# An encoder block on one core: late vectors in the pool's lowest place, b22 split one product earlier, and a rearranged last stage

## The chip, the core and the metric

One core of a Trainium2 chip runs the kernel. Its engines work side by side, each through its own queue in order: TensorE (PE, with weight loads PEld), VectorE (DVE), ScalarE (ACT), GpSimd (POOL), and SyncE (SP), which only issues DMAs. The metric is device time in microseconds (us), the median of the runs. Rows of the profile begin with the time from the span's start and the duration, both in us.

## The reference, cut to what matters

The block is an attention and a recurrence side by side, a projection with a layer norm, and a gated feed-forward part with a second norm. 1024 tokens, width 1024, everything float32. The change lies in the last two lines:

```python
h = layer_norm(DEEPNORM_ALPHA * h + merged @ w_o[l], ln1_g[l], ln1_b[l])
gate, up = jnp.split(h @ w_ffn_in[l], 2, axis=-1)          # 1024 -> 2 x 2816
h = layer_norm(DEEPNORM_ALPHA * h + (silu(gate) * up) @ w_ffn_out[l], ln2_g[l], ln2_b[l])
```

## The kernel before

**Products.** Every float32 operand is split into `hi` (a cast on ACT, L272) and `lo` (the source less `hi`, L276, on POOL for weights and often on DVE for activations). A block of a product is then three matmuls: hi by hi (L297), hi by lo (L298), lo by hi (L299), each 128 x 128 by 128 x 512. A large product is cut into 2 x 2 blocks, and seven block products are made instead of eight, with sums and differences of the blocks as operands (Strassen's scheme in Winograd's form). In the program's names b11, b12, b21 and b22 are the blocks of one side, t1 to t4 their sums, a11 to a22 the blocks of the other side and s1 to s4 theirs. `PRODUCTS` pairs them: product 5 is s1 by t1, 6 is s2 by t2, 3 is s4 by b22, 7 is s3 by t3, 4 is a22 by t4.

**The seam.** `phase2` makes the first norm's rows, tile after tile of 128 tokens. `turn(t)` transposes a tile (tsv) and `h1_blocks` makes the operands of the feed-forward product from it. For tokens 512 and up, b22, t3 and t4 go to DRAM (`td`, stores by `later` on SP) and `late_block` loads them back (`t_raw`) once their room is free; each of its four functions splits one quarter (`xb22`, `xt3`, `xt4`). `ffn_in` then runs 22 groups of seven products, one for each block of 128 gate and 128 up columns. The first two groups, g0 and g1, run in an order written by hand (`in_order`, which keeps each engine's instructions as the program has them). `Group.keep` copies a product out of PSUM (wkeep, L126, ACT), `Group.out` ends one with `evac`: fc (L1439), a tanh (fth, L1440), L1441. `Group.prep` splits a weight. Its sums (L100) are s1 and s2 in wsum and s3 and s4 in place in f_raw.

**Pools.** A pool of SBUF gives places to its tiles in the order in which they are first asked for. The pool `ffn` takes room that the pools of `phase2` had, and a tile whose place was another tile's waits for that tile's last readers. Its first tile is fc; its lowest place lies where tsum (t1, t2 and t4 before they are split or stored) was.

**The last stage.** `ffn_out` makes the second product. X and Z are four PSUM banks each; `OUT_ORDER` is (1, 2, 6, 5, 3, 7), and each of these six products goes over NJ = 11 weight blocks in 11 steps of 12 matmuls. A step s makes, in program order: `sums(s + 2)` on DVE, `prep(s + 2)` (w_hi on ACT, w_lo on POOL, four buffers of each), the loads listed for it in `bulk`, in p7 `later` (the split of t4: t4hi on ACT, t4lo on DVE), its 12 matmuls, one or two functions from `todo`, and `acts` for three steps on (ghi and glo, 256 KB each, three buffers of each). p3 and p7 name the products 3 and 7. `todo` holds what follows a product: adds of its banks to the rows Y, statistics, and in p7 the norms of the first four tiles. The last product, a22 by t4, goes tile by tile, four times 33 matmuls, with `late` (t4) against the operands A (704 KB for hi, 704 KB for lo, loaded by `last_acts`), and the norms and stores of the last four tiles follow.

Of the kernel before, what the change touches and what calls it, by code (L numbers as in the profile page):

```python
# [149 lines left out]
class Block:  # L150
# [1216 lines left out]
    def h1_blocks(self, pool, t, v, last=False):  # L1367

        nc = self.nc
        c = slice(128 * (t % 4), 128 * (t % 4) + 128)  # L1370

        def put(name, v):
            hi, lo = self.xb[name]
            self.split(hi[:, :, c], lo[:, :, c], v,
                       eng_lo="dve" if last else "pool")

        if t < 4:
            for i, n in enumerate(("b11", "b21")):
                put(n, v(i))
            return ()  # L1380

        def later(i, name, v):
            nc.sync.dma_start(self.td[i][:, :, c], v)

        def tmp():
            return pool.tile([128, 4, 128], F32, name="tsum", tag="tsum", bufs=3)

        def less(o, a, i, name):
            hi, lo = (z[:, :, c].bitcast(F32) for z in self.xb[name])
            nc.vector.tensor_sub(o, a, hi)  # L1390
            nc.vector.tensor_sub(o, o, lo)

        t1, t2 = tmp(), tmp()
        b12 = v(0)
        less(t1, b12, 0, "b11")
        put("t1", t1)
        b22 = v(1)

        def second():
            nc.vector.tensor_sub(t2, b22, t1)  # L1400
            put("t2", t2)

        def rest():
            later(0, "b22", b22)
            nc.vector.tensor_sub(b12, b22, b12)
            later(1, "t3", b12)
            hi, lo = (z[:, :, c].bitcast(F32) for z in self.xb["b21"])
            nc.vector.tensor_sub(t2, hi, t2)
            nc.vector.tensor_add(t2, t2, lo)
            later(2, "t4", t2)  # L1410

        return second, rest
# [9 lines left out]
    def ffn_in(self):  # L1422

        nc = self.nc
        with ExitStack() as es:
# [4 lines left out]
            C = {}  # L1430

# [54 lines left out]
            def vecs(v):  # L1486
                t = fp.tile([128, D], F32, name="ab", tag=f"ab{len(ab)}", bufs=1)
                nc.scalar.dma_start(t, bass.AP(tensor=v.tensor, offset=v.offset, ap=[[0, 128], [1, D]]))
                ab.append(t)

# [12 lines left out]
            with self.in_order():  # L1503
# [6 lines left out]
                splits = late_block(0)  # L1510
                g1.m5 = g1.keep(g1.product(5, 2, True))
                g0.prep(3)
                splits += late_block(1)
                g1.u2 = g1.keep(g1.product(6, 1, False))
                for f in splits[:4]:
                    f()
                g0.prep(7)
                g0.out(0, 1, g0.product(3, 2, False), g0.u2)
                for f in splits[4:]:
                    f()  # L1520
                g1.prep(3)
# [11 lines left out]
            ab = []  # L1533
            held = (g1.out(1, 0, g1.product(4, 1, False), None) for _ in range(1))
            for p in range(2, NF):
# [8 lines left out]
                if p == 3:  # L1544
                    for v in self.ln["1"]:
                        vecs(v)
# [93 lines left out]
    def ffn_out(self):  # L1640
# [3 lines left out]
        with ExitStack() as es:  # L1644
# [34 lines left out]
            def last_acts(t, i):  # L1679
                if i == 0:  # L1680
                    A.append([rp.tile([128, NJ, 128], F32R, name=f"a22{z}", tag=f"a22{z}", bufs=2) for z in "hl"])
                nc.sync.dma_start(A[t][i].bitcast(F32), self.gd["a22"][i][:, :, 128 * t:128 * (t + 1)])

            def sums(s):
# [6 lines left out]
                elif p == 6:  # L1691
                    W["t2", j] = t2 = self.ws.tile([128, HALF], F32, name="wt2", tag="wkeep", bufs=4)
                    nc.vector.tensor_sub(t2, b22, b11)
                elif p == 5:
                    nc.vector.tensor_add(b21, b21, b11)
                elif p == 7:
                    nc.vector.tensor_sub(b12, b22, b12)
                elif p == 3:
                    nc.vector.tensor_sub(b21, b21, b22)
# [25 lines left out]

            def moments(t):
                mv = self.tiny.tile([128, 4], F32, name="mv2", tag="bnmv", bufs=3)
# [3 lines left out]
                return mv  # L1731
# [4 lines left out]
            def whole(t):  # L1736
                y = Y[t]
                self.normalise(rp, y, y, moments(t))
                nc.gpsimd.tensor_mul(y, y, V[0])
                ends.append(t)  # L1740
                if len(ends) > 1:
                    end()

            ends, stores = [], []

            def end():
                t = ends.pop(0)
                nc.vector.tensor_add(Y[t], Y[t], V[1])
                stores.append(t)

            def finish(t, parts):
                y, (g2, b2), mv = Y[t], V, moments(t)
# [20 lines left out]
            for i in range(2):  # L1773
                at(46 + 2 * i, vector, i)
                for t in range(2):
# [6 lines left out]
            def later(j):  # L1782
                late[j] = [wb.tile([128, HALF], F32R, name=f"t4{z}", tag=f"{n}{j}", bufs=1)
                           for z, n in (("hi", "b11"), ("lo", "b12"))]
# [8 lines left out]
            for s, (p, j) in enumerate(steps):  # L1793
# [3 lines left out]
                with self.in_order():  # L1797
# [4 lines left out]
                    if p == 7 and j:  # L1802
                        later(j - 1)
                    self.out_step(s, *ready.pop(s))
                    for _ in range(2 if p == 7 else 1):
# [4 lines left out]
                if j == NJ - 1:  # L1810
# [10 lines left out]
                    if p == 3:  # L1821
                        todo = [a for r in range(4) for a in (todo[r], todo[4 + r])]
                        todo += [(whole, r) for r in range(4)]

            with self.in_order():
                later(NJ - 1)
                for f, *a in todo:
                    f(*a)
                end()
                for t in range(4, 8):  # L1830
                    stat(t, 1)
                for t in range(4):
# [3 lines left out]
                    if t < 2:  # L1836
                        for i in range(2):
                            last_acts(2 + t, i)
                    while stores:
                        store(stores.pop(0))  # L1840
                    if t in (1, 2):
                        whole(3 + t)
                        end()
# [43 lines left out]
```

## Time and profile before

| what | value |
|---|---|
| time, three runs | 2162.76 us median, 2158.73 to 2165.23 |
| the profiled execution's own time | 2162.12 us |
| its span | 2160.2 us |
| mean granted clock of TensorE | 0.984 |
| where it was below 1 in the parts touched | 0.90 in 1480 to 1550, 0.86 in 2071.3 to 2119.3 |

In the rows of windows the columns are the stretch, its length, the busy time of PE, PEld, DVE, ACT and POOL with the count of instructions, the granted clock, the DMA engines' share and GB/s. In rows of waits: who waited for whom, us in total, how often, the longest. In rows of groups: line, engine, operation, operands, shapes and count, then busy time and mean ns of one, then idle time before them and what ended it. In rows of the timeline the bracket is the idle time before the instruction and what ended it.

### The profile page before, as it was taken

To read this page: it belongs to the slowest core of one execution; us is meant where nothing else is said; L and a number is where in the kernel's file an instruction comes from. 1 tells how busy PE (TensorE), PEld (TensorE's weight loads), DVE (VectorE), ACT (ScalarE), POOL (GpSimd) and SP (SyncE) were. 2 spreads that over 40 slices of the span, in tenths; PEclk is the share of its full clock that TensorE was granted. 3 is DMA by queue.
4 is the path that set the end of the run, shared out by engine and by line. 5 is a ranking of instruction groups with operands and counts; after the bars stand their busy time and mean duration, and the time that the engine had idled before them with its cause. 6 is when DMAs were issued, how large, how long until landed. Compare 5 with 4: busy or idle time off the path is not lost.

```text
span 2160.2 us, 31223 instructions
## 1 busy us (share of the span) xinstructions
PE 2038.3 (94%) x10941; PEld 1678.3 (78%) x10941; DVE 1368.7 (63%) x2172; ACT 918.3 (43%) x1867; POOL 1199.0 (56%) x955
## 2 busy tenths in 40 slices
PE   4799999999999999989999899998899999999987
PEld 3678887878877888777888688886688888888866
DVE  7667646876459854768446623356767776759645
ACT  6544455444544436444364431243434344444221
POOL 3465653566436763556635864242667776755542
PEclk9899999999999999999999999999999999999999
DMA  5343442435334453333535764244445444467674
GB/s 205 102 127 103 139 148 92 148 118 159 118 95 140 137 164 103 127 118 124 162 98 179 237 219 145 78 142 146 132 146 180 138 167 150 160 213 277 212 223 132
DMA packets 296447, 324.20 MB, mean 150 GB/s; under 512 B 15905, under 2 KB 212834, under 8 KB 296290
## 3 DMA queue, kind: packets, MB, share of 16 engines
q1 hardware_dynamic: 288832, 296.81, 42.8%
q10 hardware_dynamic: 7458, 25.40, 3.0%
q8 instruction: 86, 1.41, 0.3%
q14 instruction: 71, 0.58, 0.1%
HBM read 211.78 MB, written 110.36 MB: 149 GB/s over the span
## 4 chain that ended last, share of the span: by engine, by line
PE 60%; DVE 6%; issue 5%; POOL 4%; DMA 2%; ACT 2%; SPq 0%; DVEq 0%; POOLq 0%; ACTq 0%
PE pj L297 13%; PE pj L298 12%; PE pj L299 12%; PE sd L297 6%; PE sd L298 6%; PE sd L299 5%; POOL w_lo L276 2%; PE sd L1091 1%; ACT p L869 1%; DVE hR L1052 1%; PE sd L905 1%; DVE p L891 1%; DVE hR L1051 1%; DMA a22l<-ga22l 0%; PE sd L696 0%
## 5 line engine op out<-in xcount | busy, mean ns | idle before, releaser
L276 POOL TENSOR_TENSOR w_lo<-wa,w_hi 128x512 fp32r<-128x512 f32 x276 | 386.7, 1409 | 277.0 <-ACT w_hi L272 255.1
L272 ACT CAST w_hi<-wa 128x512 fp32r<-128x512 f32 x276 | 170.1, 618 | 230.1 <-PE pj L298 162.3
L276 POOL TENSOR_TENSOR w_lo<-f_raw,w_hi 128x512 fp32r<-128x512 f32 x110 | 175.7, 1609 | 112.9 <-ACT w_hi L272 51.0
L297 PE MATMUL pj<-xt1hi,w_hi 128*128 128x512 f32 x268 | 108.6, 406 | 15.1 <-ACT xt1hi L272 6.6
L298 PE MATMUL pj<-xt1lo,w_hi 128*128 128x512 f32 x268 | 107.3, 400 | 4.5 <-DVE xt1lo L276 4.5
L299 PE MATMUL pj<-xt1hi,w_lo 128*128 128x512 f32 x268 | 106.7, 398 | 0.7 <-POOL w_lo L276 0.7
L299 PE MATMUL pj<-xb22hi,w_lo 128*128 128x512 f32 x268 | 104.9, 392 | 2.4 <-POOL w_lo L276 2.4
L297 PE MATMUL pj<-xb22hi,w_hi 128*128 128x512 f32 x268 | 105.7, 394 | 1.2 <-ACT xb22hi L272 1.2
L298 PE MATMUL pj<-xb22lo,w_hi 128*128 128x512 f32 x268 | 104.9, 392 | 0.2 <-DVE xb22lo L276 0.2
L531 POOL TENSOR_TENSOR wa<-wa,wa 128x512 f32<-128x512 f32 x46 | 64.5, 1402 | 72.6 <-DVE ws L530 55.5
L276 POOL TENSOR_TENSOR w_lo<-Wb,w_hi 128x512 fp32r<-128x512 f32 x47 | 66.2, 1410 | 68.0 <-ACT w_hi L272 63.7
L272 ACT CAST w_hi<-f_raw 128x512 fp32r<-128x512 f32 x110 | 67.9, 620 | 83.0 <-DVE f_raw L100 32.5
L276 POOL TENSOR_TENSOR w_lo<-ws,w_hi 128x512 fp32r<-128x512 f32 x46 | 67.3, 1468 | 63.0 <-ACT w_hi L272 60.8
L553 ACT COPY wkeep<-pj 128x512 f32<-128x512 f32 x138 | 80.4, 582 | 13.8 <-DVE evh L472 7.8
L276 POOL TENSOR_TENSOR w_lo<-wsum,w_hi 128x512 fp32r<-128x512 f32 x44 | 65.9, 1498 | 34.2 <-ACT w_hi L272 33.7
L297 PE MATMUL pj<-xb11hi,w_hi 128*128 128x512 f32 x188 | 77.0, 411 | 4.9 <-DVE wkeep L470 3.3
L456 DVE TENSOR_TENSOR evh<-wkeep,pj 128x512 f32<-128x512 f32 x48 | 32.7, 680 | 76.3 <-PE pj L299 56.2
L1043 ACT ACTIVATE hS<-hR,dec 128x128 f32<-128x128 f32 x112 | 44.5, 402 | 82.0 <-DVE hR L1052 58.5
L297 PE MATMUL pj<-xt4hi,w_hi 128*128 128x512 f32 x188 | 75.5, 402 | 2.9 <-DVE evh L445 2.9
L299 PE MATMUL pj<-xt2hi,w_lo 128*128 128x512 f32 x188 | 74.3, 395 | 3.4 <-POOL w_lo L276 3.4
L298 PE MATMUL pj<-xb11lo,w_hi 128*128 128x512 f32 x188 | 75.6, 402 | 1.0 <-DVE xb11lo L276 1.0
L530 DVE TENSOR_TENSOR ws<-wa,wa 128x512 f32<-128x512 f32 x46 | 38.5, 838 | 60.0 <-DMA wa<-in_w_in_dram 44.5
(423 smaller groups left out, 6629.5 us busy)
## 6 DMA issues: line engine op xcount, KB each, us to landing
wa<-in_w_in_dram SPq DMA_DIRECT2D x184, 256.0 KB, 3.0
f_raw<-in_w_ffn_in_dram SPq DMA_DIRECT2D x44, 512.0 KB, 4.2
Wb<-in_w_ffn_out_dram SPq DMA_DIRECT2D x40, 256.0 KB, 5.3
tg<-evh SPq DMA_DIRECT2D x32, 256.0 KB, 3.1
tg<-tg SPq DMA_DIRECT2D x16, 512.0 KB, 3.6
y<-ahs SPq DMA_DIRECT2D x16, 512.0 KB, 3.4
ah<-xt ACTq DMA_DIRECT2D x8, 512.0 KB, 6.4
rec<-hg ACTq DMA_DIRECT2D x8, 512.0 KB, 4.0
```

The source lines that it names most:

```text
L272: nc.scalar.copy(hi, src)
L276: e.tensor_sub(lo, src, hi.bitcast(F32))
L297: nc.tensor.matmul(ps, whi, xhi, start=first, stop=False, **kw)
L298: nc.tensor.matmul(ps, whi, xlo, start=False, stop=False, **kw)
L299: nc.tensor.matmul(ps, wlo, xhi, start=False, stop=last, **kw)
L456: nc.vector.tensor_add(t, add, ps)
L530: nc.vector.tensor_add(a["s1"], a["a21"], a["a22"])
L531: nc.gpsimd.tensor_sub(a["a21"], a["a11"], a["a21"])
L553: nc.scalar.copy(t, ps)
L869: nc.scalar.activation(z, z, AF.Exp, bias=N0[p, hd, tt:tt + 1], scale=QSCALE, accum_out=L0[p, hd, tt:tt + 1])
L891: nc.vector.tensor_scalar(z, z, W0[p, hd, tt:tt + 1], None, op0=OP.mult)
L1043: nc.scalar.activation(S[:, c, :], E, AF.Copy, scale=dec[:, 1, c:c + 1])
```

## The change

1. `h1_blocks` stores b22 as soon as it is there, no longer with t3 and t4.
2. `ffn_in` asks for the two vectors ab (gain and bias of the first norm, used from the fifth group on) before any other tile of its pool, and loads them from SP's queue instead of ACT's.
3. In the hand-written order b22 and t3 are split one product earlier than before, and g0's third weight is prepared before g1's product 5.
4. In the last stage the sums of product 7 are made with those of product 5; t4 is split in p3 instead of p7 (its `lo` goes to b22's place, no longer to b12's); the norm of a tile is cut into moments, normal, gained and total, which `todo` interleaves over four tiles, three functions per step of p7; A has three buffers instead of two, and the third tile's operands are loaded in p7.

```diff
         b22 = v(1)
+        later(0, "b22", b22)
...
         def rest():
-            later(0, "b22", b22)
             nc.vector.tensor_sub(b12, b22, b12)
...
             C = {}
+            ab = [fp.tile([128, D], F32, name="ab", tag=f"ab{i}", bufs=1) for i in range(2)]
...
                 splits = late_block(0)
+                g0.prep(3)
                 g1.m5 = g1.keep(g1.product(5, 2, True))
-                g0.prep(3)
                 splits += late_block(1)
-                g1.u2 = g1.keep(g1.product(6, 1, False))
                 for f in splits[:4]:
                     f()
+                g1.u2 = g1.keep(g1.product(6, 1, False))
                 g0.prep(7)
-                g0.out(0, 1, g0.product(3, 2, False), g0.u2)
                 for f in splits[4:]:
                     f()
+                g0.out(0, 1, g0.product(3, 2, False), g0.u2)
...
                 if p == 3:
-                    for v in self.ln["1"]:
-                        vecs(v)
+                    for t, v in zip(ab, self.ln["1"]):
+                        nc.sync.dma_start(t, bass.AP(tensor=v.tensor, offset=v.offset, ap=[[0, 128], [1, D]]))
...
-                    A.append([rp.tile([128, NJ, 128], F32R, name=f"a22{z}", tag=f"a22{z}", bufs=2) for z in "hl"])
+                    A.append([rp.tile([128, NJ, 128], F32R, name=f"a22{z}", tag=f"a22{z}", bufs=3) for z in "hl"])
...
                 elif p == 5:
                     nc.vector.tensor_add(b21, b21, b11)
-                elif p == 7:
                     nc.vector.tensor_sub(b12, b22, b12)
...
+            def normal(t):
+                self.normalise(rp, Y[t], Y[t], MV[t])
+
+            def gained(t):
+                nc.gpsimd.tensor_mul(Y[t], Y[t], V[0])
+
+            def total(t):
+                nc.vector.tensor_add(Y[t], Y[t], V[1])
+                stores.append(t)
...
-                for t in range(2):
+                for t in range(3):
                     at(52 + 4 * t + 2 * i, last_acts, t, i)
...
-                           for z, n in (("hi", "b11"), ("lo", "b12"))]
+                           for z, n in (("hi", "b11"), ("lo", "b22"))]
...
-                    if p == 7 and j:
-                        later(j - 1)
+                    if p == 3:
+                        later(j)
                     self.out_step(s, *ready.pop(s))
-                    for _ in range(2 if p == 7 else 1):
+                    for _ in range(3 if p == 7 else 1):
...
-                        todo += [(whole, r) for r in range(4)]
+                        for k in range(7):
+                            todo += [(f, k - n) for n, f in ((3, total), (2, gained), (1, normal), (0, moments))
+                                     if 0 <= k - n < 4]
...
-                    if t < 2:
+                    if t == 0:
                         for i in range(2):
-                            last_acts(2 + t, i)
+                            last_acts(3, i)
```

The first place is the seam. On SP, the queue before, from the store of tile 6's b22 (td_199 is b22, td_200 t3, td_201 t4):

```order
L1383 DMA td_199<-tsv 512x1x128
L1383 DMA td_200<-tsv 512x1x128
L1383 DMA td_201<-tsum 512x1x128
L1383 DMA td_199<-tsv 512x1x128
L1383 DMA td_200<-tsv 512x1x128
L1383 DMA td_201<-tsum 512x1x128
L1496 DMA t_raw<-td_199 128x512 x4
L1496 DMA t_raw<-td_200 128x512 x4
L1496 DMA t_raw<-td_201 128x512 x4
```

And the same place of the changed kernel:

```order
L1383 DMA td_199<-tsv 512x1x128 x2
L1383 DMA td_200<-tsv 512x1x128
L1383 DMA td_201<-tsum 512x1x128
L1383 DMA td_200<-tsv 512x1x128
L1383 DMA td_201<-tsum 512x1x128
L1492 DMA t_raw<-td_199 128x512 x4
L1492 DMA t_raw<-td_200 128x512 x4
L1541 DMA ab<-in_ln_g_dram 128x1024
L1541 DMA ab<-in_ln_b_dram 128x1024
L1492 DMA t_raw<-td_201 128x512 x4
```

Tile 7's b22 goes ahead of the four stores of t3 and t4, and the two vectors now stand before the last four loads.

On ACT, at the same place, before (the second row is the tanh of g0's first evacuation, the fourth the weight of g1's product 5):

```order
L1488 DMA ab<-in_ln_g_dram 128x1024
L1440 ACTIVATE fth<-fc 128x512
L126 COPY wkeep<-pj 128x512
L1488 DMA ab<-in_ln_b_dram 128x1024
L272 CAST w_hi<-wsum 128x512
L126 COPY wkeep<-sd 128x512
L1440 ACTIVATE fth<-fc 128x512
L272 CAST w_hi<-wsum 128x512
L126 COPY wkeep<-sd 128x512
L272 CAST w_hi<-f_raw 128x512
L126 COPY wkeep<-pj 128x512
L272 CAST xb22hi<-t_raw 128x512 x4
```

And of the changed kernel, from the same tanh:

```order
L1441 ACTIVATE fth<-fc 128x512
L126 COPY wkeep<-pj 128x512
L272 CAST w_hi<-wsum 128x512
L126 COPY wkeep<-sd 128x512
L1441 ACTIVATE fth<-fc 128x512
L272 CAST w_hi<-wsum 128x512
L272 CAST w_hi<-f_raw 128x512
L126 COPY wkeep<-sd 128x512
L272 CAST xb22hi<-t_raw 128x512 x4
L126 COPY wkeep<-pj 128x512
L272 CAST w_hi<-f_raw 128x512
L272 CAST xt3hi<-t_raw 128x512 x4
```

The casts of b22 moved ahead of the copy of g1's product 6 (wkeep<-pj), those of t3 ahead of the tanh that follows product 3; on DVE the halves xt3lo moved ahead of that product's fc in the same way.

The second place is product 7 of the last stage. ACT before, where the norms begin (Wb_17805 to Wb_17886 are weights of p7, the other Wb are blocks of t4, y rows of a tile):

```order
L272 CAST w_hi<-Wb_17805 128x512
L272 CAST t4hi<-Wb_17673 128x512
L320 ACTIVATE y_17888<-y_17888,mv_18963 128x1024
L320 ACTIVATE y_17915<-y_17915,mv_18970 128x1024
L272 CAST w_hi<-Wb_17832 128x512
L272 CAST t4hi<-Wb_17699 128x512
L320 ACTIVATE y_17942<-y_17942,mv_19003 128x1024
L320 ACTIVATE y_17969<-y_17969,mv_19011 128x1024
L272 CAST w_hi<-Wb_17859 128x512
L272 CAST t4hi<-Wb_17726 128x512
L272 CAST w_hi<-Wb_17886 128x512
```

And of the changed kernel:

```order
L272 CAST w_hi<-Wb_17778 128x512
L320 ACTIVATE y_17888<-y_17888,mv_18954 128x1024
L272 CAST w_hi<-Wb_17805 128x512
L320 ACTIVATE y_17915<-y_17915,mv_18981 128x1024
L272 CAST w_hi<-Wb_17832 128x512
L320 ACTIVATE y_17942<-y_17942,mv_19008 128x1024
L272 CAST w_hi<-Wb_17859 128x512
L320 ACTIVATE y_17969<-y_17969,mv_19039 128x1024
L272 CAST w_hi<-Wb_17886 128x512
```

The t4 casts left p7, and one norm's activation stands between two weights instead of two.

POOL of the changed kernel at that place (mv is a column of moments raised to -1/2, the y rows are `gained`):

```order
L1726 TENSOR_TENSOR mv_18954<-mv_18954,mhalf 128x1
L276 TENSOR_TENSOR w_lo<-Wb_17778,w_hi 128x512
L1726 TENSOR_TENSOR mv_18981<-mv_18981,mhalf 128x1
L1732 TENSOR_TENSOR y_17888<-y_17888,gb_18661 128x1024
L276 TENSOR_TENSOR w_lo<-Wb_17805,w_hi 128x512
L1726 TENSOR_TENSOR mv_19008<-mv_19008,mhalf 128x1
L276 TENSOR_TENSOR w_lo<-Wb_17832,w_hi 128x512
L1732 TENSOR_TENSOR y_17915<-y_17915,gb_18661 128x1024
L1726 TENSOR_TENSOR mv_19039<-mv_19039,mhalf 128x1
L276 TENSOR_TENSOR w_lo<-Wb_17859,w_hi 128x512
```

Before, two multiplies and two columns stood between one weight and the next; now at most one multiply does.

More of the change, by code (lines that the diff above doesn't have):

```diff
@@ L1484, in combine @@
                     parts("s4", j, s4)
[L1486 to L1489, printed above, removed]
             self.first_evac = [evac_of(FS[p]) for p in range(2)]
@@ L1532, in ffn_in @@
             combine(0, 0)
-            ab = []
             held = (g1.out(1, 0, g1.product(4, 1, False), None) for _ in range(1))
@@ L1724, in stat @@
                 nc.vector.bn_stats(S[t][:, h, :], Y[t][:, halves[h]])
+            MV = {}
             def moments(t):
-                mv = self.tiny.tile([128, 4], F32, name="mv2", tag="bnmv", bufs=3)
+                MV[t] = mv = rp.tile([128, 4], F32, name="mv2", tag=f"mv{t}", bufs=1)
                 nc.vector.bn_aggr(mv[:, 0:2], S[t])
@@ L1730, in moments @@
                 nc.gpsimd.tensor_tensor(mv[:, 2:3], mv[:, 2:3], self.mhalf[:, 0:1], OP.pow)
-                return mv
+            def normal(t):
[5 more added lines that the diff above has]
+                stores.append(t)
             def store(t, c=slice(0, D)):
                 nc.sync.dma_start(self.out[128 * t:128 * (t + 1), c], Y[t][:, c])
[L1736 to L1749, printed above, removed]
+            stores = []
             def finish(t, parts):
-                y, (g2, b2), mv = Y[t], V, moments(t)
+                moments(t)
+                y, (g2, b2), mv = Y[t], V, MV[t]
                 for s in parts:
@@ L1822, in ffn_out @@
                         todo = [a for r in range(4) for a in (todo[r], todo[4 + r])]
-                        todo += [(whole, r) for r in range(4)]
+                        for k in range(7):
+                            todo += [(f, k - n) for n, f in ((3, total), (2, gained), (1, normal), (0, moments))
+                                     if 0 <= k - n < 4]
             with self.in_order():
-                later(NJ - 1)
                 for f, *a in todo:
                     f(*a)
-                end()
                 for t in range(4, 8):
@@ L1841, in ffn_out @@
                     if t in (1, 2):
-                        whole(3 + t)
-                        end()
+                        for f in (moments, normal, gained, total):
+                            f(3 + t)
                     if t == 3:
```

## The prediction, made before the changed kernel was run

> **What bounds the kernel now.** I read the page first, then the windows, then the waits of the stretches in which PE is not full.
>
> ```profile
> span 2160.2 us, 31223 instructions
> PE 2038.3 (94%) x10941; PEld 1678.3 (78%) x10941; DVE 1368.7 (63%) x2172; ACT 918.3 (43%) x1867; POOL 1199.0 (56%) x955
> PE   4799999999999999989999899998899999999987
> GB/s 205 102 127 103 139 148 92 148 118 159 118 95 140 137 164 103 127 118 124 162 98 179 237 219 145 78 142 146 132 146 180 138 167 150 160 213 277 212 223 132
> ```
>
> PE is the bound: 94% busy, and full in most of the 40 slices. An edit can gain only where PE is not full. The change touches two such places: the seam between the output projection and the feed-forward stage (slices 27 to 29) and the last 90 us. The windows give what lies in each.
>
> ```profile
> 1480.00:1550.00 70.00, 54.03 (x202) 39.90 (x201) 47.50 (x60) 26.76 (x50) 30.58 (x22) 0.90 0.45 137
> 1970.00:2040.00 70.00, 70.00 (x311) 57.96 (x310) 51.07 (x57) 24.11 (x41) 37.44 (x28) 1.00 0.65 212
> 2066.00:2088.00 22.00, 21.79 (x94) 17.08 (x93) 13.05 (x18) 5.81 (x10) 7.76 (x6) 1.00 1.00 303
> 2071.30:2119.30 48.00, 35.91 (x133) 26.92 (x133) 28.39 (x43) 15.65 (x23) 23.12 (x16) 0.86 0.48 151
> 2119.30:2152.50 33.20, 30.71 (x134) 24.48 (x132) 14.81 (x25) 2.49 (x2) 7.33 (x5) 1.00 0.61 198
> ```
>
> The second row is PE at its pace: 70 us for 311 matmuls, 0.225 us each, so a product of 12 takes 2.70 us and one of 132 takes 29.7. The fourth row is the seventh product of the last stage, called p7 below: 132 matmuls in 48.0 us, 18.3 too long. The fifth is the last product, also 132: 33.2 us, 3.5 too long. In the first row 202 matmuls took 70 us instead of 45.5: 24.5 us lost, some of them to transposes that stay. These three are all that the change can win.
>
> **The seam.** These are the rows of the engines there.
>
> ```profile
> 1495.60 0.69 DVE L1409 TENSOR_TENSOR tsum<-tsum,xb21lo 128x512 f32<-128x512 f32 x1
> 1499.98 0.69 DVE L1439 TENSOR_TENSOR fc<-wkeep,sd 128x512 f32<-128x512 f32 x1 [3.69 <-DMA td<-tsum]
> 1503.41 0.80 PE L297 MATMUL sd<-xt1hi,w_hi 128*128 128x512 f32 x1 [5.63 <-ACT w_hi L272]
> 1503.44 1.28 POOL L276 TENSOR_TENSOR w_lo<-wsum,w_hi 128x512 fp32r<-128x512 f32 x1 [10.36 <-ACT w_hi L272]
> 1506.60 1.28 POOL L276 TENSOR_TENSOR w_lo<-wsum,w_hi 128x512 fp32r<-128x512 f32 x1 [1.88 <-ACT w_hi L272]
> 1513.25 0.51 PE L297 MATMUL pj<-xb22hi,w_hi 128*128 128x512 f32 x1 [1.25 <-ACT xb22hi L272]
> 1516.81 0.69 DVE L1439 TENSOR_TENSOR fc<-wkeep,pj 128x512 f32<-128x512 f32 x1 [1.08 <-PE pj L299]
> 1518.80 2.49 DVE L276 TENSOR_TENSOR xt3lo<-t_raw,xt3hi 128x512 fp32r<-128x512 f32 x4
> 1522.68 1.29 POOL L276 TENSOR_TENSOR w_lo<-f_raw,w_hi 128x512 fp32r<-128x512 f32 x1 [5.81 <-ACT w_hi L272]
> 1526.42 0.39 PE L297 MATMUL pj<-xt3hi,w_hi 128*128 128x512 f32 x1
> ```
>
> The first fc, in the pool's lowest place, waits for two stores that still read tsum there; DVE was free at 1495.60 + 0.69 = 1496.3. With the vectors in that place no row of the changed order waits for them: 3.7 us. Everything hung on that fc shifts with it: the product of group 1 with xt1 starts at 1499.7, its w_lo (1504.72) is there at 1501.0 and the next product's (1507.88) at 1504.2. From each w_lo ten matmuls remain: 1501.0 + 2.25 = 1503.3, and 1504.2 + 2.25 = 1506.5. The b22 split now runs one product earlier, from about 1503.9 (behind a copy of the product that ends at 1503.3), so it hides beside the product that ends at 1506.5. Group 0's third product follows without its 1.25 us: 1509.2. The t3 split starts behind one copy and one cast (about 0.6 each, as the casts quoted further down), at about 1507.7, and is ready as PE needs it: group 0's seventh ends at 1511.9.
>
> What is late next is group 1's third product. Its weights hang on the evacuation of the product that ends at 1509.2, and that evacuation now stands behind xt3lo on DVE, which ends at about 1507.7 + 0.6 + 2.5 = 1510.8. Before, from the start of that fc (1516.81) to the end of the w_lo (1523.97) was 7.2 us with 2.4 of xt3lo inside: 4.8 without. So w_lo is there at 1515.6 and the product ends at 1517.9, against 1526.42 before: 8.5 us won. Behind it the same chain of POOL's halves and weight loads sets the pace as before, shifted. Against this stand the clock's windows:
>
> ```profile
> 1488.40:1491.85 3.45, 1.73 (x6) 1.16 (x7) 2.25 (x3) 2.61 (x6) 1.74 (x2) 1.00 0.57 195
> 1491.85:1495.25 3.40, 3.40 (x9) 2.60 (x8) 3.37 (x5) 0.00 (x0) 1.23 (x1) 0.51 0.45 131
> PE pj L297 <- ACT w_hi L272: 1.1, 1, 1.1
> ```
>
> A window in which PE was half idle was followed by one at 0.51 of the clock: 9 matmuls where 15 fit. Two such idle spells stay (1497.8 to 1501.0, 1511.9 to 1515.6). Each can cost up to 1.7 us, part of it under the chain's own waits; I take 1.2 for both: **7.3 us**. Ends: 4 (both windows in full, and a later split) to 8.5. [...]
>
> The two vector loads move from ACT's queue to SP's, ahead of the last four t_raw loads. 2 x 512 KB at 303 GB/s is 3.5 us of transfer; those t_raw wait anyway for the b22 halves (about 1507) and are cast at about 1519. Behind the two on SP stand only those loads and the next weights, which wait for POOL longer. Cost 0; without that cover 3.5.
>
> **The seventh product.** Here are its waits, two matmuls behind the longest of them, two t4lo in a row on DVE, its groups and the load of a last operand.
>
> ```profile
> ACT w_hi L272 <- DVE Wb L1697: 15.5, 7, 3.4
> PE pj L297 <- ACT w_hi L272: 6.8, 2, 3.8
> PE pj L298 <- POOL w_lo L276: 4.9, 2, 2.6
> 2095.81 0.59 PE L297 MATMUL pj<-w_hi,ghi 128*128 128x512 f32 x1 [3.85 <-ACT w_hi L272]
> 2106.56 0.80 PE L297 MATMUL pj<-w_hi,ghi 128*128 128x512 f32 x1 [2.99 <-ACT w_hi L272]
> 2072.72 1.29 DVE L276 TENSOR_TENSOR t4lo<-Wb,t4hi 128x512 fp32r<-128x512 f32 x1 [1.35 <-ACT t4hi L272]
> 2077.29 1.30 DVE L276 TENSOR_TENSOR t4lo<-Wb,t4hi 128x512 fp32r<-128x512 f32 x1 [1.35 <-ACT t4hi L272]
> L276 DVE TENSOR_TENSOR t4lo<-Wb,t4hi 128x512 fp32r<-128x512 f32 x11 | 12.7, 1172 | 10.5 <-ACT t4hi L272 10.5
> L276 POOL TENSOR_TENSOR w_lo<-Wb,w_hi 128x512 fp32r<-128x512 f32 x8 | 11.2, 1396 | 14.6 <-ACT w_hi L272 14.6
> L1739 POOL TENSOR_TENSOR y<-y,gb 128x1024 f32<-128x1024 f32 x4 | 10.0, 2488 | 6.2 <-ACT y L320 6.2
> a22h<-ga22h SPq DMA_DIRECT2D x4, 704.0 KB, 6.7
> ```
>
> ACT's w_hi waits 15.5 us for the sums (L1697), which stand on DVE behind t4lo and behind norms that wait for POOL. Two steps of 10.75 us came of it. The change takes 11 sums, 11 t4hi and 11 t4lo out of p7, so a w_hi waits only for its buffer; four buffers let it run two to three steps ahead. What remains in one queue with it is one normalise on ACT and one multiply on POOL per step. A POOL step with a multiply holds 1.4 + 2.5 = 3.9 us, over 2.70, but only four of 11 are such: 11 x 1.4 + 4 x 2.5 = 25.4 of 29.7 us, beside four one-column operations. Walking POOL's order by these durations, the last w_lo ends some 26 us into p7, and its step starts at 27.0. So PE has no wait on an engine left: 18.3.
>
> What is late next is DMA. Each step loads 2 x 256 KB; the last operands, 704 KB each, come at every second step, now six of them instead of four. The window 2066 to 2088 held just this mix, at share 1.00 and 303 GB/s. Two steps are 4 x 0.262 + 0.721 = 1.77 MB, 5.84 us against 5.40: 0.44 per pair, six pairs, 2.6 us. Ends: 0, if the three buffers take it, and 6 at the 277 GB/s of the page's best slice (6.4 us per pair). **Gain 18.3 - 2.6 = 15.7.**
>
> **Where the moved work goes.** The sums go to the fifth product, the t4 splits to p3, the product before p7.
>
> ```profile
> 2039.44 2.73 DVE L1719 TENSOR_TENSOR y<-y,sd 128x512 f32<-128x512 f32 x4 [17.00 <-PE sd L299]
> 2042.09 8.80 DVE L1699 TENSOR_TENSOR Wb<-Wb,Wb 128x512 f32<-128x512 f32 x9
> L276 POOL TENSOR_TENSOR w_lo<-Wb,w_hi 128x512 fp32r<-128x512 f32 x11 | 15.6, 1422 | 14.3 <-ACT w_hi L272 14.3
> L272 ACT CAST w_hi<-Wb 128x512 fp32r<-128x512 f32 x11 | 6.8, 622 | 23.1 <-PE sd L299 23.1
> ```
>
> In the fifth product DVE idles 17.00 us before the adds that free the bank for p3; 11 sums of 0.98, the pace of the second row, are 10.8: hidden, and beyond 17 us they would hold p3. In p3 (the last two rows, 2041 to 2071) ACT idles 23.1 us and takes 11 casts of 0.62, 6.8; DVE takes 11 halves of 1.17, 12.9, beside 8.8 of sums, in 29.7. No wait is added that PE sees: t4lo needs the cast just before it and b22's w_lo of two steps ago. Cost 0 to 4, taken 0.
>
> **The last product.** Its third operand now is loaded before it starts and the fourth after its first quarter.
>
> ```profile
> PE pj L299 <- DMA a22l<-ga22l: 1.5, 1, 1.5
> PE pj L297 <- DMA a22h<-ga22h: 0.9, 1, 0.9
> 2152.51 0.69 DVE L1719 TENSOR_TENSOR y<-y,pj 128x512 f32<-128x512 f32 x1 [5.36 <-PE pj L299]
> ```
>
> The fourth pair is then issued 15 us before use and ahead of the stores. Both waits go, with the slow restarts the 3.5 us of the window; DVE idled 5.36 us before its last add, which covers 3.5. **Gain 3.5**, ends 1 and 3.5.
>
> **The sum.** The profiled execution took 2162.12 us, 1.9 more than its span and 0.6 below the median shown. 7.3 + 15.7 + 3.5 = 26.5: **2135.6 us**.
>
> **Rivals.**
> The clock stays up in the seam: 1.2 us more won, 2134.4. [...] Chance 0.14.
> DMA is worse: 6 us of stalls instead of 2.6, 2139.0; for it the full share, against it the 303 GB/s held for 22 us. 0.11.
> p3 is paced by DVE and POOL together: their operations lengthen beside each other (t4lo 1.17 on the mean, a sum 0.98, w_lo 1.42). One after the other they make 3.57 per step, 0.87 over 2.70; 9.6 in 11 steps, less two steps of lead, 4.2: 2139.8. Chance 0.09. [...]
> The norms still hold w_hi once (the change does not do what it says): one step of 10.75 stays, 8 us: 2143.6. Chance 0.07.
> The seam's gain is eaten by the chain behind it, by weight loads that wait for DMA: 2142.9. Chance 0.05.
> The slower side: in p3 ACT and DVE fall into lockstep. Before, in p7, two t4lo stood 4.57 us apart with sum and cast between them. At that period p3 loses 11 x 1.87 = 20.6 less three steps of lead, 8.1, so 12.5: 2148 (0.02). From about 5.3 us per step the time is within 0.3% of before (0.02), from 6.4 on it is slower by more, at 8 us 2186 (0.03). Against it: w_hi in p3 needs no sum.
>
> **How the numbers follow.** Forecast 0.47; the rivals as given. The range 2129 to 2147 reaches from every term at its best (8.5 + 18.3 + 3.5, 2131.8) to the norms' rival at 2143.6, each with 3 us for the scatter of the runs shown. A change of 0.3%, 6.5 us, is about what a measurement of this kernel can tell: faster 0.95, within 0.02, slower 0.03.
>
> **What would show it.** In the seam: the first fc about 0.6 us behind the last tsum, no wait of PE for xb22hi or xt3hi, and PE waiting instead for group 1's weights. In p7: no wait of ACT's w_hi for a sum, about 32 us in all, small waits of PE for ghi and glo. In the last product: no wait for a22. Wrong would be p3 longer than 30 us, a step of p7 over 5 us, or an fc that still waits for a store.

## The result, and the profile after

| | before | after |
|---|---|---|
| median of the runs, us | 2162.27 (2158.73 to 2165.23, 4 runs) | 2137.1 (2136.52 to 2137.73, 4 runs) |
| ratio | 1 | 0.9884, 95% interval 0.9867 to 0.9901 |
| profiled execution and its span, us | 2162.12, 2160.2 | 2136.52, 2134.7 |

The change made the kernel faster by 1.2%. In all medians and ratios here, three executions of the kernel before that took 35% longer or more are left out. The profiled executions differ by 25.6 us, where the prediction had 26.5. The page of the changed kernel begins so (span, busy time by engine, PE's 40 slices):

```profile
span 2134.7 us, 31233 instructions
PE 2030.1 (95%) x10941; PEld 1674.5 (78%) x10941; DVE 1375.5 (64%) x2172; ACT 916.8 (43%) x1867; POOL 1199.1 (56%) x955
PE   4799999999999999989999899999899999999998
```

PE's instructions are the same 10941. Its last slices are full now. The windows of the two places, columns as before (stretch; its length, then busy time and count of PE, PEld, DVE, ACT, POOL; clock; DMA share; GB/s):

```profile
1480.00:1550.00 70.00, 58.46 (x228) 44.62 (x228) 51.85 (x64) 31.01 (x58) 35.39 (x25) 0.93 0.51 161
2065.90:2097.00 31.10, 31.08 (x132) 24.13 (x133) 18.92 (x24) 9.41 (x12) 24.25 (x16) 1.00 0.88 273
2097.00:2127.00 30.00, 30.00 (x133) 24.60 (x131) 13.58 (x24) 2.49 (x2) 7.39 (x5) 1.00 0.49 172
```

In the seam 228 matmuls ran in 70 us instead of 202. P7 takes 31.1 us instead of 48.0, the last product 30.0 instead of 33.2. The whole list of PE's waits from 2000 us to the end is one row, and ACT's list in p7 has no sum any more (line waiting, what it waits for: us in total, times, longest):

```profile
PE sd L299 <- DMA glo<-gs4l: 0.4, 1, 0.4
...
ACT y L320 <- DVE mv L319: 6.7, 3, 3.0
ACT w_hi L272 <- PE pj L299: 5.8, 3, 2.6
ACT w_hi L272 <- PE sd L299: 2.1, 1, 2.1
```

A w_hi now waits for PE alone, that is, for a free buffer: the engine that works ahead waits for the one that is the bound. The time line of the seam, rows of DVE, PE and POOL in order of time:

```profile
1495.39 0.69 DVE L1409 TENSOR_TENSOR tsum<-tsum,xb21lo 128x512 f32<-128x512 f32 x1
1496.00 0.68 DVE L1440 TENSOR_TENSOR fc<-wkeep,sd 128x512 f32<-128x512 f32 x1
1499.43 0.50 PE L297 MATMUL sd<-xt1hi,w_hi 128*128 128x512 f32 x1 [1.88 <-ACT w_hi L272]
1509.42 3.18 DVE L276 TENSOR_TENSOR xt3lo<-t_raw,xt3hi 128x512 fp32r<-128x512 f32 x4 [0.68 <-ACT xt3hi L272]
1512.52 0.67 DVE L1440 TENSOR_TENSOR fc<-wkeep,pj 128x512 f32<-128x512 f32 x1
1515.95 0.50 PE L297 MATMUL sd<-xb22hi,w_hi 128*128 128x512 f32 x1 [2.31 <-ACT w_hi L272]
1515.97 1.66 POOL L276 TENSOR_TENSOR w_lo<-f_raw,w_hi 128x512 fp32r<-128x512 f32 x1 [5.73 <-ACT w_hi L272]
1541.60 0.50 PE L299 MATMUL pj<-xb22hi,w_lo 128*128 128x512 f32 x1 [0.88 <-POOL w_lo L276]
```

The first fc runs 0.61 us behind the last tsum, without a wait. PE waits for neither xb22hi nor xt3hi; the long wait is for the weights of group 1's third product, as foreseen. The last row is the mark that serves as the seam's end below; it stood at 1547.62.

The seam starts at 1478.3 to 1482.6 us in the runs below, whatever the kernel, so they are compared by four stretches of PE's time line: **seam**, from the first transposes that wait for y (1480.76 before, 1480.56 after) to that mark; **middle**, from there to p7's first matmul (2071.31, 2065.92); **p7**, to the first matmul with t4 (2119.39, 2097.00); **last**, to the last matmul (2152.09, 2126.70). Before: 66.9, 523.7, 48.1, 32.7. After: 61.0, 524.3, 31.1, 29.7. So -5.8, +0.6, -17.0 and -3.0 make -25.2 of the span's -25.5; 0.2 lie ahead of the seam, 0.1 behind the last matmul.

The stretches come from one profiled execution of each kernel, and kernels that are alike in a stretch show how far they can be trusted. Over the numbers above and the table below, the six kernels with the changed seam have 60.5 to 61.9 us in it, the five with the old last stage 523.7 to 524.7 in the middle, and the five with the change's p7 31.1 to 32.4 there. A difference of about 1 us between two kernels can't be told from this scatter.

### The profile page after: what moved, and what is told of

Read it like the earlier page. It is cut to its first block, busy times and chain, and to the rows that moved or that the text cites. A ratio compares the mean times of both kernels' runs of the same rounds, so it can differ in the third digit from the quotient of the medians.

```text
span 2134.7 us, 31233 instructions
## 1 busy us (share of the span) xinstructions
PE 2030.1 (95%) x10941; PEld 1674.5 (78%) x10941; DVE 1375.5 (64%) x2172; ACT 916.8 (43%) x1867; POOL 1199.1 (56%) x955
## 4 chain that ended last, share of the span: by engine, by line
PE 59%; DVE 5%; POOL 4%; issue 4%; DMA 3%; ACT 1%; SPq 0%; DVEq 0%; ACTq 0%; POOLq 0%
PE pj L297 12%; PE pj L299 12%; PE pj L298 12%; PE sd L299 6%; PE sd L298 6%; PE sd L297 5%; POOL w_lo L276 3%; PE sd L1091 1%; DVE hR L1052 1%; DMA wa<-in_w_in_dram 1%; DVE hR L1051 1%; DVE qd L1006 0%; DMA binb<-in_ln_in_b_dram 0%; POOL att_lo L276 0%; PE sd L696 0%
## 5 line engine op out<-in xcount | busy, mean ns | idle before, releaser
L297 PE MATMUL pj<-xt1hi,w_hi 128*128 128x512 f32 x268 | 108.8, 407 | 16.4 <-ACT xt1hi L272 8.0
L272 ACT CAST w_hi<-f_raw 128x512 fp32r<-128x512 f32 x110 | 67.9, 620 | 82.7 <-DVE f_raw L100 31.7
L456 DVE TENSOR_TENSOR evh<-wkeep,pj 128x512 f32<-128x512 f32 x48 | 32.7, 681 | 76.1 <-PE pj L299 54.8
```

The lines of the kernel that those rows point to most:

```text
L272: nc.scalar.copy(hi, src)
L297: nc.tensor.matmul(ps, whi, xhi, start=first, stop=False, **kw)
L456: nc.vector.tensor_add(t, add, ps)
```

## The experiments

Every kernel computes all that the reference asks for. Ratios are to the kernel before, timed beside it; its medians were 2163.65, 2164.86 and 2163.76 us in the three groups of runs. The last four columns are the stretches just defined.

| run | median, us | ratio, 95% interval | seam | middle | p7 | last |
|---|---|---|---|---|---|---|
| seam_alone | 2157.13 | 0.9972 (0.9960 to 0.9984) | 60.9 | 524.7 | 48.5 | 33.1 |
| last_alone | 2144.32 | 0.9904 (0.9889 to 0.9918) | 66.6 | 524.2 | 31.7 | 29.7 |
| place_alone | 2164.77 | 1.0001 (0.9992 to 1.0010) | 67.5 | 523.7 | 48.1 | 32.3 |
| splits_alone | 2161.49 | 0.9988 (0.9980 to 0.9997) | 63.7 | 523.9 | 48.1 | 33.2 |
| place_and_queue | 2161.06 | 0.9991 (0.9982 to 1.0000) | 63.8 | 523.8 | 48.1 | 33.0 |
| norms_whole | 2147.63 | 0.9920 (0.9903 to 0.9937) | 61.0 | 523.3 | 42.4 | 29.7 |
| t4_in_p7 | 2145.92 | 0.9917 (0.9900 to 0.9934) | 61.9 | 523.4 | 40.7 | 29.8 |
| both_in_p7 | 2155.22 | 0.9953 (0.9935 to 0.9972) | 61.1 | 524.4 | 48.1 | 29.7 |
| two_bufs | 2142.62 | 0.9896 (0.9879 to 0.9913) | 60.5 | 523.7 | 30.9 | 35.7 |
| weights3_early | 2138.09 | 0.9888 (0.9875 to 0.9902) | 61.8 | 524.2 | 31.3 | 29.7 |
| weights5_early | 2137.72 | 0.9891 (0.9875 to 0.9907) | 63.3 | 523.5 | 31.6 | 29.7 |
| weights_all_early | 2139.77 | 0.9896 (0.9883 to 0.9910) | 61.7 | 525.6 | 32.4 | 29.7 |

### The two halves of the change

The first kernel takes `h1_blocks` and `ffn_in` of the change with the old `ffn_out`, the second the new `ffn_out` with the old rest.

> The kernel before with the seam's three edits alone (vectors in the pool's lowest place, b22's store first, splits one product earlier); the last stage stays as it was. Theory (the parts add, and the seam is worth what the changed kernel's seam showed, 6.0 us at the matmul where the chain of weights ends, 1547.62 before against 1541.60): 2156.2 us, the seventh product of the last stage still 48 us, starting some 6 us earlier. Rival (the seam's gain is lost in the 500 us of full PE behind it): within 1 us of before, 2162.

> The kernel before with the last stage's edits alone (sums in the fifth product, t4 halves in p3, norms in steps, three late operands); the seam stays as it was. Theory (the parts add): 25.6 - 6.0 = 19.6 us less, 2142.7 us; p7 31 us, last product 30 us. Rival (a part of the last stage's gain needs the earlier start that the seam gives): 2145 to 2150 us.

Measured -6.0 and -20.8 us by the timings (0.28% and 0.96% of 2163.65), and by the stretches 5.9 in the seam of the one, 16.4 and 3.0 in p7 and last of the other. The halves add within the intervals: the seam's gain is not lost in the 500 us of full PE, and the last stage needs no earlier start.

### The place, the queue and the splits

place_alone moves the tiles and leaves their loads on ACT's queue:

```diff
             C = {}
+            ab = [fp.tile([128, D], F32, name="ab", tag=f"ab{i}", bufs=1) for i in range(2)]
...
-            def vecs(v):
-                t = fp.tile([128, D], F32, name="ab", tag=f"ab{len(ab)}", bufs=1)
+            def vecs(t, v):
                 nc.scalar.dma_start(t, bass.AP(tensor=v.tensor, offset=v.offset, ap=[[0, 128], [1, D]]))
```

> The kernel before with one edit: the two vectors take the pool's lowest place, first of all; they are loaded where they were, on ACT's queue, and every split stays in its old order. Theory: the first fc starts at about 1496.1 instead of 1499.98, all of the chain behind it shifts by that, the b22 split too (its loads land by about 1503): 3.7 us less, 2158.6 us. Rival (b22's halves are what is late next, since their store and loads do not shift): the product with b22 waits longer on xb22hi, 1.5 us less at most, 2160.8 us.

Both were wrong: it won nothing. In its time line fc has lost its wait, and the tanh behind it has got one (ACT and ACT's DMA queue):

```profile
1497.82 0.68 DVE L1440 TENSOR_TENSOR fc<-wkeep,sd 128x512 f32<-128x512 f32 x1
...
1501.64 0.34 ACTq L1488 DMA_DIRECT2D ab<-in_ln_g_dram  x1
1502.02 0.63 ACT L1441 ACTIVATE fth<-fc 128x512 f32<-128x512 f32 x1 [9.17 <-DMA td<-tsum]
1502.08 0.39 ACTq L1488 DMA_DIRECT2D ab<-in_ln_b_dram  x1
```

The loads of ab take over the place, so they take over the wait for the stores of tsum. On ACT's queue the first of them stands ahead of the tanh, which is ready at 1498.5 and starts at 1502.02, when the load has been issued: the wait was handed from DVE to ACT. The row names the store, not the load that carries it; the load is seen only as the row just ahead in the queue. One word tells whether it is the queue:

```diff
-                nc.scalar.dma_start(t, bass.AP(tensor=v.tensor, offset=v.offset, ap=[[0, 128], [1, D]]))
+                nc.sync.dma_start(t, bass.AP(tensor=v.tensor, offset=v.offset, ap=[[0, 128], [1, D]]))
```

> The kernel before with the vectors in the pool's lowest place and their loads issued by SP, as in the change, and nothing else: every split stays in its old order. It differs from the run that moved the place alone in the loads' queue only. Theory (in that run the loads, which now wait for the two stores, stood on ACT's queue ahead of the first tanh, so the wait only went from DVE to ACT: fc ran at 1497.82 without a wait and fth waited 9.17 us): on SP nothing queues behind them that is due, the first matmul of group 1's fifth product starts 18.9 us after the first transposes that wait for y instead of 22.6, and the kernel is 3.4 us faster than before (what the seam's 6.0 leaves beside the 2.6 of the splits alone). Rival (the t_raw loads behind them on SP, or b22's late store, take the gain): that matmul starts early, but the product with b22 waits longer and the seam ends within 1 us of before.

```profile
1497.62 0.68 DVE L1440 TENSOR_TENSOR fc<-wkeep,sd 128x512 f32<-128x512 f32 x1
...
1498.34 0.63 ACT L1441 ACTIVATE fth<-fc 128x512 f32<-128x512 f32 x1 [5.68 <-DVE fc L1440]
...
1501.05 0.79 PE L297 MATMUL sd<-xt1hi,w_hi 128*128 128x512 f32 x1 [3.52 <-ACT w_hi L272]
```

The tanh follows fc at once, and the fifth product of group 1 starts 1501.05 - 1482.16 = 18.9 us after the first transposes, as expected. The seam is 3.1 us shorter than before (by the timings 1.9, interval 0 to 3.9). The third part alone, b22's store and the splits with fc in its old place:

> The kernel before with b22's store first and the splits one product earlier, but fc still in the pool's lowest place, so that the first fc waits for the two stores. Theory (the two effects add): the rest of the seam's 6.0, 2.1 us less, 2160.2 us, with no wait of PE for xb22hi and xt3hi and a wait for group 1's weights in their place. Rival (the splits do nothing while fc is late): 2162.3 us. The other rival (the splits alone win all, fc's wait being hidden): 2156 us.

Its loads of ab are on SP's queue too. It measured 3.2 us in the seam, 2.6 by the timings: the theory's side, with a little more. 3.1 and 3.2 make 6.3 beside the 6.0 of all three edits, so these two effects add, but the first of them exists only as place **and** queue. The queue by itself was not run. In the kernel before it has nothing to win at this point: there fc ends at 1500.67 and the tanh starts at 1500.70.

### What held p7

Three edits left p7 at once. norms_whole puts `whole` back, with two entries of the list per step; t4_in_p7 puts `later(j - 1)` back into p7; both_in_p7 puts the sums back too. An excerpt of the last:

```diff
                 elif p == 5:
                     nc.vector.tensor_add(b21, b21, b11)
+                elif p == 7:
                     nc.vector.tensor_sub(b12, b22, b12)
...
-                    if p == 3:
-                        later(j)
+                    if p == 7 and j:
+                        later(j - 1)
```

> The changed kernel with the first four norms of the last stage in one piece again (moments, normalise and multiply of a row block in one go, two entries of the list per step), while the sums stay in the fifth product and the t4 halves in p3. Theory (two things held w_hi in p7, the sum it casts and the normalise that stands ahead of it on ACT and waits for DVE and POOL): with the sum gone the norms still hold ACT for two steps, p7 takes 36 to 44 us instead of 31.1, the kernel 2142 to 2150 us. Rival (only the sums held w_hi, the steps of the norms were not needed): p7 stays within 1.5 us of 31.1, 2137 to 2138.5 us.

> The changed kernel with the t4 halves back in p7, one per step behind the seventh product's casts; the sums stay in the fifth product, the norms in steps. Theory (t4lo cost p7 only because the sums stood behind it): DVE is then about full in p7 (18.2 us busy in the changed kernel, plus 11 x 1.17 = 12.9), its norms get late, but no w_hi needs DVE except through a normalise on ACT; p7 31 to 34 us, 2137 to 2140 us. Rival (the t4 halves themselves set p7's step): p7 about 40 us, 2146 us.

> The changed kernel with both the sums and the t4 halves back in p7, as before the change, and only the norms in steps. Theory (w_hi waits for a sum that stands on DVE behind t4lo and the norms' pieces; the first two t4lo of p7 before the change stood 4.57 us apart): p7 40 to 46 us, 2146 to 2152 us. Rival (the norms in one piece were the whole cost): p7 31 to 32 us, 2137 us.

Norms in one piece cost 11.3 us of p7, inside the theory's bounds. Here is ACT there:

```profile
2079.37 1.25 ACT L320 ACTIVATE y<-y,mv 128x1024 f32<-128x1024 f32 x1 [3.21 <-DVE mv L319]
2080.53 0.60 ACT L272 CAST w_hi<-Wb 128x512 fp32r<-128x512 f32 x1
2085.06 1.25 ACT L320 ACTIVATE y<-y,mv 128x1024 f32<-128x1024 f32 x1 [3.93 <-DVE mv L319]
2089.47 1.24 ACT L320 ACTIVATE y<-y,mv 128x1024 f32<-128x1024 f32 x1 [3.17 <-DVE mv L319]
2090.62 1.64 ACT L272 CAST w_hi<-Wb 128x512 fp32r<-128x512 f32 x3
```

Two normalise steps between one w_hi and the next make 10.1 us, with no sum in p7 at all. The steps of 10.75 us before the change had the same hold in them, as ACT's rows of the kernel before show:

```profile
2095.14 0.62 ACT L272 CAST w_hi<-Wb 128x512 fp32r<-128x512 f32 x1 [0.57 <-DVE Wb L1697]
2095.66 0.61 ACT L272 CAST t4hi<-Wb 128x512 fp32r<-128x512 f32 x1
2099.64 1.24 ACT L320 ACTIVATE y<-y,mv 128x1024 f32<-128x1024 f32 x1 [3.37 <-DVE mv L319]
2104.08 1.24 ACT L320 ACTIVATE y<-y,mv 128x1024 f32<-128x1024 f32 x1 [3.19 <-DVE mv L319]
2105.89 0.62 ACT L272 CAST w_hi<-Wb 128x512 fp32r<-128x512 f32 x1 [0.57 <-DVE Wb L1697]
```

From one w_hi to the next 10.75 us pass. The two normalise steps wait 3.37 and 3.19 of them, the sum only 0.57.

The t4 halves cost 9.6 us, and there the theory fell: the rival's 40 us came. ACT and DVE of that run, around one step:

```profile
2086.45 0.60 ACT L272 CAST w_hi<-Wb 128x512 fp32r<-128x512 f32 x1
2086.96 0.62 ACT L272 CAST t4hi<-Wb 128x512 fp32r<-128x512 f32 x1
2087.61 1.40 DVE L276 TENSOR_TENSOR t4lo<-Wb,t4hi 128x512 fp32r<-128x512 f32 x1 [2.04 <-ACT t4hi L272]
2088.94 3.42 DVE L1735 TENSOR_TENSOR y<-y,gb 128x1024 f32<-128x1024 f32 x1
2092.28 0.15 DVE L319 SCALAR_TENSOR_TENSOR mv<-mv 128x1 f32<-128x1 f32 x1
2092.47 1.24 ACT L320 ACTIVATE y<-y,mv 128x1024 f32<-128x1024 f32 x1 [4.89 <-DVE mv L319]
2093.61 0.60 ACT L272 CAST w_hi<-Wb 128x512 fp32r<-128x512 f32 x1
```

This is a ring through two queues: w_hi, then t4hi on ACT, then t4lo, total and the norm's column on DVE, then normalise on ACT, and only behind it the next w_hi: 7.16 us in this turn, 6.02 in the one before (w_hi at 2080.43). It needs no sum; t4lo only has to stand ahead of the column on DVE while the normalise stands ahead of w_hi on ACT. ACT's normalise waits 14.5 us in this run's list (14.5, 4 times, longest 4.9), against 6.7 in the changed kernel.

With both back, the norms in steps alone bring nothing: p7 is 48.1 us, the value of before, and the kernel 2155.2, beyond the theory's 2152. Its waits of ACT in p7:

```profile
ACT w_hi L272 <- DVE Wb L1692: 13.9, 4, 6.6
ACT y L320 <- DVE mv L319: 13.3, 4, 4.9
```

So the 17 us are no sum of three terms. Out of p7's 48.1, the steps alone win 0, both moves alone 48.1 - 42.4 = 5.7, the steps with the sums' move 48.1 - 40.7 = 7.4, and all together 17.0. In these runs w_hi came on time only where ACT's queue was free of all three. Which hold lasts longest with the sums alone in p7 (norms in steps, t4 in p3) was not run.

### The last operands

```diff
-                A.append([rp.tile([128, NJ, 128], F32R, name=f"a22{z}", tag=f"a22{z}", bufs=3) for z in "hl"])
+                A.append([rp.tile([128, NJ, 128], F32R, name=f"a22{z}", tag=f"a22{z}", bufs=2) for z in "hl"])
...
-                    if t == 0:
+                    if t < 2:
                         for i in range(2):
-                            last_acts(3, i)
+                            last_acts(2 + t, i)
```

> The changed kernel with two buffers for the last operands instead of three: the third and fourth are loaded after the first and second quarter of the last product, as before the change. Theory (each of these waits was the product's own): the waits for a22h and a22l come back, 0.9 + 1.5 us and the slow restarts, last product 32 to 33.2 us instead of 29.7, and p7, with 2 x 0.72 MB less to load, at most 1 us shorter than 31.1; 2138.5 to 2140 us. Rival (the waits came of the stores of the late norms, which now are out of the way): last product 30 us, 2136.5 us.

The waits came back, larger than expected: the last product took 35.7 us. PE's waits in it, and the window behind the longest:

```profile
PE pj L299 <- DMA a22l<-ga22l: 2.7, 2, 1.5
PE pj L297 <- DMA a22h<-ga22h: 1.0, 1, 1.0
...
2126.30:2129.70 3.40, 3.40 (x13) 2.66 (x13) 0.00 (x0) 0.00 (x0) 0.00 (x0) 0.79 0.39 155
```

3.7 us of waits and slow stretches make 6.0. Before the change the same loads, issued as long after the product's start (7.45 and 14.9 us), left 0.9 + 1.5 us of waits; the wait that comes on top here is 1.1 us for the third tile's a22l. It is no effect of the new last stage: seam_alone, with the old one, has it too (0.9 us, last product 33.1). So it comes in some runs and not in others, and why stays open; in the five kernels with the old last product, which has two buffers, it took 32.3 to 33.2 us. The greater part of the rest is pace: behind the last wait seven matmuls came 0.42 to 0.59 us apart here, 1.6 us more than at 0.227, and before the change 0.23 to 0.33 apart. P7 was 0.2 us shorter with 2 x 0.72 MB less to load, which is inside the scatter: no cost of the third pair of operands shows in p7.

### What is late next in the seam

Three kernels prepare group 1's weights earlier on top of the change, to win its remaining waits. weights3_early:

```diff
                 g0.prep(7)
+                g1.prep(3)
                 for f in splits[4:]:
                     f()
                 g0.out(0, 1, g0.product(3, 2, False), g0.u2)
-                g1.prep(3)
```

weights5_early sets `g1.prep(5)` and `g1.prep(6)` ahead of `g0.out(0, 0, ...)` and `g1.out(0, 0, ...)`; weights_all_early does both, and sets `g1.prep(7)` ahead of `g0.out(1, 1, ...)`.

> The changed kernel with group 1's third weights prepared (sum on DVE, cast on ACT, half on POOL) ahead of the t3 splits instead of behind group 0's third evacuation. Theory (that product is what is late next in the seam, since its weights stand behind xt3lo, fc and fth on DVE): its waits of 2.31 and 1.01 us go, and with them the window at 0.53 of the clock behind them, 10 matmuls in 3.40 us instead of 15, 1.1 us; 3.5 us less (2 to 4.4), 2133.6 us. Rival (the t4 halves or group 0's seventh are as late, so the waits only move): within 1 us of 2137.

> The changed kernel with group 1's fifth and sixth weights prepared ahead of the two first evacuations instead of behind each. Theory (the sum for them then runs at 1496.0 on DVE, 2.0 us earlier, and fc 0.6 later): group 1's fifth product waits 0.4 us or less for w_hi and w_lo instead of 1.88 + 0.62, PE is over half busy in the 3.4 us there, and the window at 0.54 of the clock behind it (10 matmuls in 3.40 us, 1.1 us lost) goes; 2 to 3.6 us less in the seam, 2134.2 us. Rival (b22's halves, whose loads land at about 1503, are late then): PE waits for xb22hi again and the kernel gains under 1 us.

> Both of the other two runs' edits on the changed kernel, and group 1's seventh weights ahead of group 0's seventh evacuation. Theory (the seam is a chain of weights behind evacuations, and each link moved wins its own wait): the two gains add, 5 to 8 us less, 2131 us, no window of the seam under 0.9 of the clock. Rival (one gain only, since the loads of the t vectors, which wait for their buffers, set the pace behind): 2133.5 to 2135 us.

None beats the changed kernel (0.9884), and the three theories fail. The rivals of the first two hold in the main: the waits moved, though in weights5_early PE waits for xb22lo and not for xb22hi. In weights_all_early the rival's 2133.5 to 2135 us did not come either. In weights3_early the wait for group 1's third weights did go, and one as long came two products later:

```profile
1525.82 0.69 DVE L100 TENSOR_TENSOR wsum<-f_raw 128x512 f32<-128x512 f32 x1 [3.40 <-DMA f_raw<-in_w_ffn_in_dram]
1526.43 1.29 DVE L276 TENSOR_TENSOR xt4lo<-t_raw,xt4hi 128x512 fp32r<-128x512 f32 x2
...
1527.17 0.50 PE L298 MATMUL sd<-xt4lo,w_hi 128*128 128x512 f32 x1 [3.89 <-DVE xt4lo L276]
```

The scheduler set a sum of group 2, which waits for a weight load, further up on DVE, ahead of the first two xt4lo instead of behind them; PE waits for xt4lo behind it. In weights5_early the same sum waits 1.56 us there, and PE waits for xb22lo besides (1.4 us); its fifth product did start 2.0 us earlier, but waited 1.50 and 0.63 us for w_hi and w_lo, and seven matmuls behind that came 0.42 to 0.43 us apart. So the run does not show whether the clock stays up when PE is over half busy in such a spell. In weights_all_early PE's waits are spread over xb22, xt3 and xt4, 1.9 us the longest, and the seam is 61.7. The seams of this run and of weights3_early are inside the scatter of the changed seam, that of weights5_early (63.3) is longer. A kernel that also holds that sum back was not run.

## Why the prediction was right

It gave 2135.6 us in 2129 to 2147; 2137.1 was measured. The places and what holds them were right; some sizes and one cause were not. By its own steps:

**The seam**, 7.3 predicted, 5.8 measured. The mechanism was right in each row named there, and two sizes were off. w_lo for group 1's third product was set at 1515.6; it ended at 1515.97 + 1.66 = 1517.63, mostly since xt3lo started 1.1 us later and took 3.18 us instead of 2.5. From there to the next product 4.0 us passed instead of 2.25. Those 2.0 and 1.8 us are what the foreseen 8.5 lost. And "I take 1.2 for both" idle spells was too little:

```profile
1498.00:1501.40 3.40, 1.35 (x4) 0.85 (x5) 2.24 (x5) 1.64 (x3) 1.28 (x1) 0.95 0.93 231
1501.40:1504.80 3.40, 3.40 (x10) 2.62 (x10) 1.09 (x2) 1.24 (x2) 2.19 (x2) 0.54 0.98 307
...
1515.00:1518.40 3.40, 1.45 (x5) 0.86 (x6) 1.48 (x3) 0.62 (x1) 2.43 (x2) 0.96 0.00 0
1518.40:1521.80 3.40, 3.40 (x10) 2.71 (x9) 0.00 (x0) 0.62 (x1) 1.74 (x2) 0.53 0.00 0
```

Both spells, PE 40 and 43% busy, were followed by a window at half the clock with 10 matmuls where 15 fit: 3.40 - 10 x 0.227 = 1.1 us each, 2.3 together; the first spell's part lies ahead of that w_lo, in its lateness. The rival in which the clock stays up is out: behind spells in which PE's longest waits were 1.88 and 2.31 us the clock was 0.54 and 0.53. Not every half idle window had such a one behind it: in weights_all_early a window with PE 45% busy (1528.6 to 1532.0) was followed by one at 1.00. So of the 8.5 us foreseen at the end of that product 4.75 were there (1526.42 against 1521.67, where PE starts the next product); the chain behind it, said to be only "shifted", then won another 1.3, partly since its two waits for xt4lo fell from 0.38 and 1.86 to 0.90 and 0.61.

**The queue** was called a cost of 0. The number was right and the role was missed: without that move the place wins nothing. The prediction took each edit's cost alone; the runs show a condition between two.

**P7**, 15.7 predicted, 17.0 measured. The DMA's 2.6 was the mis-sized term: what is above 132 x 0.227 = 30.0 us is 1.1. PE's own list has no wait for DMA in p7; the weight loads have small ones, as foreseen, and PE's pace breaks by 0.1 to 0.2 us at five of the six:

```profile
PEld pj L299 <- DMA glo<-gs3l: 1.7, 6, 0.3
```

In the four other kernels with this p7 PE itself waits 0.2 to 1.2 us for ghi, and p7 takes 31.3 to 32.4 us, so part of the 1.3 us is the luck of one profile. The window is at 273 GB/s and share 0.88, below the 303 at which the prediction set the limit; of the six loads of last operands that the prediction paired with p7's steps, the first two are issued in p3 (2058.33 and 2063.78). The sentence "Two steps of 10.75 us came of it" put them down to w_hi's wait for the sums. That was a misreading: in those steps the sum held w_hi for 0.57 us and the norms held ACT. The t4 halves hold it by themselves too, as t4_in_p7 shows. The 18.3 came right because it was taken for all three edits together, and that is in part luck: with one edit fewer, 9.6 or 11.3 of the 17.0 us were not there.

**Moved work**, 0 predicted, +0.6 measured in the middle, which is inside the scatter. One sign of being wrong, p3 longer than 30 us, did show: its 132 matmuls took 30.9 us against 30.0 before. PE's only wait there is 0.4 us for glo, a load, and the pace breaks for 0.7 us in all around it; without such a wait p3 took 29.9 in norms_whole. So neither the rival of DVE and POOL pacing p3 nor that of the lockstep there came. **The last product**, 3.5 predicted, 3.0 measured, by the mechanism named: two_bufs brings it back, and more.

The seam's 1.5 too much and p7's 1.3 too little nearly cancel; with 0.6 in the middle and 0.5 in the last product 1.3 of the 26.5 did not come. That the total came so close is in part the luck of these two errors.

## What to carry to other kernels

In this kernel the tiles put into a place that others still read took over the wait for them, and carried it into the queue that first wrote the tiles: on ACT's queue the tanh waited 9.17 us, on SP's it started 0.04 us behind fc. So moving a tile and choosing the queue of its load are one edit. Where an engine serves the bound from a strict queue, look at everything ahead of the serving instruction: several holds hide behind one another. Here, taking away one of three (the norms in one piece) won nothing, and putting back the norms or the t4 halves cost more than half of the whole; only a run for each tells. When a wait of the bound is taken away, read what is issued next on the same queue before counting it, since a scheduler may put another wait there, as the sum in weights3_early that waited 3.40 us.

## What was not expected of the hardware

A column operation of one element per partition on DVE took as long as a whole multiply on POOL, 2.35 us beside 2.40. Rows of the changed kernel in p7:

```profile
2071.69 0.16 DVE L319 SCALAR_TENSOR_TENSOR mv<-mv 128x1 f32<-128x1 f32 x1 [2.18 <-POOL mv L1726]
...
2074.41 2.35 DVE L319 SCALAR_TENSOR_TENSOR mv<-mv 128x1 f32<-128x1 f32 x1 [2.25 <-POOL mv L1726]
...
2074.35 2.40 POOL L1732 TENSOR_TENSOR y<-y,gb 128x1024 f32<-128x1024 f32 x1
```

The same operation took 0.16 us beside an idle POOL and 2.35 us when POOL's multiply had started 0.06 us ahead of it; both ended within 0.01 us of each other. An operation in the ring of t4_in_p7 grew beside a multiply of POOL too: the total that took 1.23 us at 2079.48 of that run took 3.42 at 2088.94, where POOL's multiply had started 0.51 us ahead of it:

```profile
2088.43 2.85 POOL L1732 TENSOR_TENSOR y<-y,gb 128x1024 f32<-128x1024 f32 x1
```
